# Hybrid decoder trunk: constant matmuls ahead of the first data, two weight groups in one walk, and upper weights against both parts of the activations in one matmul

## The chip, the core and the metric

The kernel runs on one core of a Trainium2 chip. The metric is device time in microseconds of that core; the median of three runs is given. TensorE (PE) multiplies, VectorE (DVE) and ScalarE (ACT) do the elementwise work, GpSimd (POOL) a little of it, and SyncE (SP) issues nearly all transfers. A profile is one execution, recorded by the hardware.

## What is computed

One layer over 256 tokens of width 2048, in float32, with three branches that are gated and merged:

```python
h = rmsnorm(x, ln_in_g)
proj = h @ w_in                                   # 2048 x 19472
conv_a, conv_b, conv_z, q, k, v, gla_z, alpha_lr, mq, mz, gate_pre = split(proj)
u = causal_depthwise_conv(conv_a * sigmoid(conv_b), dw_w, dw_b)        # 31 taps
u = silu(layernorm(u)) * silu(conv_z);  y_conv = u @ w_conv_out + b_conv_out
log_a = log_sigmoid(alpha_lr @ w_alpha2 + b_alpha) / 16
o = rmsnorm(gla_chunked(q * 256**-0.5, k, v, log_a))                   # 4 heads
y_gla = (o * silu(gla_z)) @ w_gla_out
om = softmax(mq @ mk.T * 128**-0.5) @ mv          # 4 heads, 256 memory tokens
y_mem = (om * silu(mz)) @ w_mem_out
g = sigmoid(gate_pre + b_gate)
out = rmsnorm(x + (g0 * y_conv + g1 * y_gla + g2 * y_mem) @ w_out)
```

## The kernel before, in words

**Products.** Weights and activations are each split into an upper part of 12 significant bits (`hi`, `xh`) and the rest (`lo`, `xl`), both as fp32r; a product is three matmuls, upper by upper, upper by lower and lower by upper (`mm3`, L157 to L160). Weights come in groups of 512 columns, 53 groups in all, in the order in which they are used. A group is walked in chunks of two k (tiles of 128 features), 512 KB each (`chunks`, `chunk`): one transfer on SP's queue into one of four `raw` tiles, a cast on ACT to `hi` (L140), a subtraction on DVE to `lo` (L141), five tiles of each. These three are put ahead of other work in the order (`high_priority`).

**Two kinds of group.** `group_n` (tokens on partitions) has activations as the stationary operand and 512 columns of weights moving: 96 matmuls of 512 columns. `group_t` (features on partitions, tiles named pt_...) has 128 columns of weights stationary and the 256 tokens moving: for each k and each of four feature tiles a triple of 256 columns, 192 matmuls, summed in two PSUM tiles [128, 2, 256]. PSUM has five such tiles for the groups (`mm_tile`) and three for the rest (`aux_tile`). The 19 transposed groups are conv a and b (four times, `conv_group`), q and k (twice, `qk_group`), the memory's keys mk, and mq and mz (`memory_groups`), and the four of conv z (`gated_conv`). What uses a finished group reads the PSUM tile directly, 512 columns at a time.

**Activations.** `raw_operand` loads xt (features on partitions, 2 MB) four tiles at a time as the first group asks for them, on SP's queue between the weights, and splits each with the gain of the norm (L187, L188). The first four groups, conv a 0, conv b 0 and q and k of the first half, use these not yet normalized activations (XR), and their results are multiplied by `xrb`, the tokens' 1/rms, which a side task (`x_norm`) makes from squares meanwhile. From v on, the normalized X is used (`xh`, `xl`). The first group starts with two chunks of one k (256 KB). The constants `idents` and `tap` are loaded on SP after conv a 0 (L457 to L459).

**Order.** Everything between the groups (the 480 tap steps of the convolution, L359, the four heads, the memory attention, the norms) is a generator that is advanced at each chunk (`tick`), with a credit of 1.2 a tick; the order on TensorE is written at the end of the kernel. From this program order and the priorities a planner fixes each engine's order before the run. It may bring later work of an engine forward when what stands ahead isn't ready by its own clock.

## Time and profile before

| | us |
|---|---|
| median of three runs | 1248.16 |
| lowest and highest run | 1247.41, 1248.22 |
| span of the profiled execution | 1246.8 |
| PE busy in it | 1231.0 |
| DVE busy in it | 964.0 |
| ACT busy in it | 591.8 |

The span runs from the first to the last instruction; a run's time has about 1.4 us more around it. Each matmul has a record; the time from one start to the next is what it costs in a row of matmuls, and its recorded duration is longer, since matmuls overlap. A matmul on plain float32 has two records.

### The profile page before, as it was taken

Reading aid. Unit: us, or ns where it says so; the run is one execution under the profiler, and the core shown is the slowest. Engines: PE = TensorE matmul, PEld = TensorE weight load, DVE = VectorE, ACT = ScalarE, POOL = GpSimd, SP = SyncE. Lnnn points to the kernel's source line nnn. Section 1 sums busy time; section 2 is a strip of 40 time slices with the busy share of each in tenths; the row PEclk is TensorE's granted clock in tenths of the full one; section 3 lists DMA queues with packets and bytes.
Section 4 is the critical chain, followed back from the end, with each engine's and each line's share of the span. In section 5 each row is a group of like instructions: output and inputs, shape, how many; then the busy total and the mean of one; then the engine's idle time right before and its main releaser. Section 6 shows DMA issues by size and latency. Waiting matters only on the chain.

```text
span 1246.8 us, 18825 instructions
## 1 busy us (share of the span) xinstructions
PE 1231.0 (99%) x7338; PEld 1093.9 (88%) x7338; DVE 964.0 (77%) x1502; ACT 591.8 (47%) x711; POOL 18.6 (1%) x29
## 2 busy tenths in 40 slices
PE   7999999999999999999999999999999999999997
PEld 7999899988998998889988888888999888888885
DVE  7999999699999667999699979964565554655553
ACT  7534676446553454444445445544354444444442
POOL 0000000000020000000000000000000000000000
PEclk9999999999999999999999999999999999999999
DMA  7565745446545445665465555565555655567562
GB/s 272 186 191 170 236 153 195 155 161 221 188 165 193 159 152 183 205 204 193 161 218 171 200 201 171 179 228 194 195 183 190 202 202 195 205 227 268 187 215 71
DMA packets 71672, 238.37 MB, mean 191 GB/s; under 512 B 7792, under 2 KB 12144, under 8 KB 71584
## 3 DMA queue, kind: packets, MB, share of 16 engines
q1 hardware_dynamic: 71440, 237.13, 56.6%
q8 instruction: 57, 0.93, 0.3%
q14 instruction: 31, 0.25, 0.1%
q10 hardware_dynamic: 144, 0.05, 0.0%
HBM read 235.06 MB, written 2.10 MB: 190 GB/s over the span
## 4 chain that ended last, share of the span: by engine, by line
PE 97%; DMA 1%; DVE 1%; issue 0%; SPq 0%; ACT 0%; POOLq 0%; DVEq 0%; POOL 0%
PE pt_cb L158 2%; PE pt_cz L158 2%; PE pt_cb L159 2%; PE pt_cb L160 2%; PE pt_cz L159 2%; PE pt_cz L160 2%; PE pn_gc L159 2%; PE pn_gm L159 2%; PE pn_gz L158 2%; PE pn_go L159 2%; PE pn_go L158 2%; PE pn_gm L158 2%; PE pn_gz L159 2%; PE pn_yo L158 2%; PE pn_go L160 2%; PE pn_gc L160 2%
## 5 line engine op out<-in xcount | busy, mean ns | idle before, releaser
L359 DVE SCALAR_TENSOR_TENSOR conv<-u,tap,conv 128x256 f32<-128x256 f32 x480 | 207.3, 474 | 0.0
L158 PE MATMUL pt_ca<-xh,hi_ca 128*128 128x256 f32 x256 | 72.7, 289 | 6.1 <-ACT xh L187 5.1
L159 PE MATMUL pt_ca<-xl,hi_ca 128*128 128x256 f32 x256 | 73.5, 288 | 0.2
L160 PE MATMUL pt_ca<-xh,lo_ca 128*128 128x256 f32 x256 | 72.7, 287 | 0.9 <-DVE lo_ca L141 0.9
L158 PE MATMUL pt_cb<-xh,hi_cb 128*128 128x256 f32 x256 | 72.4, 283 | 0.0
L141 DVE TENSOR_TENSOR lo_yc<-raw_yc,hi_yc 128x1024 fp32r<-128x1024 f32 x32 | 39.2, 1225 | 42.9 <-ACT hi_yc L140 42.9
L160 PE MATMUL pt_cz<-xh,lo_cz 128*128 128x256 f32 x256 | 71.9, 281 | 0.0
L158 PE MATMUL pt_cz<-xh,hi_cz 128*128 128x256 f32 x256 | 71.9, 281 | 0.0
L159 PE MATMUL pt_cz<-xl,hi_cz 128*128 128x256 f32 x256 | 71.9, 281 | 0.0
L160 PE MATMUL pt_cb<-xh,lo_cb 128*128 128x256 f32 x256 | 71.8, 282 | 0.0
L159 PE MATMUL pt_cb<-xl,hi_cb 128*128 128x256 f32 x256 | 71.8, 281 | 0.0
L141 DVE TENSOR_TENSOR lo_cz<-raw_cz,hi_cz 128x1024 fp32r<-128x1024 f32 x32 | 39.2, 1224 | 35.7 <-ACT hi_cz L140 35.7
L141 DVE TENSOR_TENSOR lo_gc<-raw_gc,hi_gc 128x1024 fp32r<-128x1024 f32 x32 | 39.1, 1223 | 34.2 <-ACT hi_gc L140 34.2
L141 DVE TENSOR_TENSOR lo_out<-raw_out,hi_out 128x1024 fp32r<-128x1024 f32 x32 | 39.0, 1224 | 31.5 <-ACT hi_out L140 31.2
L140 ACT CAST hi_gc<-raw_gc 128x1024 fp32r<-128x1024 f32 x32 | 33.6, 1052 | 50.3 <-PE pn_yc L160 24.9
L140 ACT CAST hi_yc<-raw_yc 128x1024 fp32r<-128x1024 f32 x32 | 33.7, 1053 | 49.5 <-PE pn_gc L160 33.4
L140 ACT CAST hi_yo<-raw_yo 128x1024 fp32r<-128x1024 f32 x32 | 33.6, 1051 | 46.7 <-PE pn_go L160 23.4
L141 DVE TENSOR_TENSOR lo_yo<-raw_yo,hi_yo 128x1024 fp32r<-128x1024 f32 x32 | 38.8, 1221 | 21.6 <-ACT hi_yo L140 21.6
L158 PEld LDWEIGHTS pt_ca<-xh,hi_ca 128*128 128x128 f32 x256 | 49.5, 196 | 6.4 <-ACT xh L187 5.1
L140 ACT CAST hi_gm<-raw_gm 128x1024 fp32r<-128x1024 f32 x32 | 33.6, 1050 | 45.2 <-PE pn_gm L160 24.6
L140 ACT CAST hi_go<-raw_go 128x1024 fp32r<-128x1024 f32 x32 | 33.7, 1052 | 44.6 <-PE pn_yo L160 24.6
L140 ACT CAST hi_cz<-raw_cz 128x1024 fp32r<-128x1024 f32 x32 | 33.6, 1050 | 44.3 <-PE pt_cz L159 36.0
(352 smaller groups left out, 4108.9 us busy)
## 6 DMA issues: line engine op xcount, KB each, us to landing
raw_cb<-in_weights SPq DMA_DIRECT2D x32, 512.0 KB, 3.5
raw_gm<-in_weights SPq DMA_DIRECT2D x32, 512.0 KB, 3.2
raw_gz<-in_weights SPq DMA_DIRECT2D x32, 512.0 KB, 3.3
raw_go<-in_weights SPq DMA_DIRECT2D x32, 512.0 KB, 3.6
raw_yo<-in_weights SPq DMA_DIRECT2D x32, 512.0 KB, 3.2
raw_cz<-in_weights SPq DMA_DIRECT2D x32, 512.0 KB, 3.2
raw_gc<-in_weights SPq DMA_DIRECT2D x32, 512.0 KB, 3.2
raw_yc<-in_weights SPq DMA_DIRECT2D x32, 512.0 KB, 3.2
```

Source lines behind the costliest of these rows:

```text
L140: nc.scalar.copy(hi, raw)
L141: nc.vector.tensor_sub(lo, raw, hi.bitcast(F32))
L158: nc.tensor.matmul(o, lhsT=ah, rhs=bh, start=first, stop=False, skip_group_check=True)
L159: nc.tensor.matmul(o, lhsT=ah, rhs=bl, start=False, stop=False, skip_group_check=True)
L160: nc.tensor.matmul(o, lhsT=al, rhs=bh, start=False, stop=last, skip_group_check=True)
L359: nc.vector.scalar_tensor_tensor(acc, u[:, i, j:j + T], tap[:, c, j:j + 1], acc, op0=ALU.mult, op1=ALU.add)
```

## The change

Four things are done.

1. Nine matmuls of a constant tile with itself are put first on TensorE; nothing reads their result. The load of the per-feature vectors gets the same priority.
2. x is loaded at once at the start, in five transfers on ACT's queue; `idents` and `tap` go to POOL's queue.
3. The first two groups, conv a 0 and conv b 0, are walked together (`group_pair`): a chunk is one k of both, 512 KB, for 24 matmuls of 256 columns, into four PSUM tiles.
4. The other 17 transposed groups are walked in two halves of 256 columns, each in four chunks of four k (512 KB again). The two parts of an activation tile lie side by side (`xs`), and the upper weights meet both in one matmul of 512 columns; the lower weights meet the upper part in one of 256. A PSUM tile then holds for one feature tile two sums, which `total` adds: a copy on ACT and an addition on DVE, at the end of each half, before the former use. In conv groups b now comes before a, so that the gate is ready when a is. The scale of q is put into the copies of v.

```diff
-NU, LAG, HELD, XWAIT = 2, 2, 12, 4
+NU, LAG, HELD, XWAIT = 2, 2, 12, 5
+WARM = 9
...
-    def chunks(w, cols, nk, acts, name, first=CK, spare=False):
+    def chunks(w, cols, nk, acts, name, first=CK, spare=False, size=CK):
         if not isinstance(cols, list):
             cols = [(cols, GC)]
         k = 0
         while k < nk:
-            ck = min(CK, first) if k < 2 * first else CK
+            ck = min(size, first) if k < 2 * first else size
...
-    def group_t(w, c0, acts, nk, name, first=CK):
-        pss = [mm_tile(f"pt_{name}_{j}") for j in range(2)]
-        for k, hi, lo, ah, al in chunks(w, c0, nk, acts, name, first):
-            for n in range(4):
-                cols = slice(n * P, (n + 1) * P)
-                mm3(pss[n // 2][:, (n % 2) * T:(n % 2 + 1) * T], hi[:, cols], lo[:, cols], ah, al,
+    def group_t(w, c0, acts, nk, name, use):
+        for h in range(2):
+            pss = [mm_tile(f"pt_{name}_{2 * h + j}") for j in range(2)]
+            cols = [(c0 + h * GC // 2, GC // 2)]
+            for k, hi, lo, ah, al, both in chunks(w, cols, nk, acts, f"{name}_{h}", 2 * CK, size=2 * CK):
+                for n in range(2):
+                    c = slice(n * P, (n + 1) * P)
+                    nc.tensor.matmul(pss[n], lhsT=hi[:, c], rhs=both, start=k == 0, stop=False,
+                                     skip_group_check=True)
+                    nc.tensor.matmul(pss[n][:, 0:T], lhsT=lo[:, c], rhs=ah, start=False, stop=k == nk - 1,
+                                     skip_group_check=True)
+            for n in range(2):
+                use(2 * h + n, pss[n][:, 0:T], pss[n][:, T:2 * T])
+    def group_pair(w, c0, c1, acts, nk, name):
+        pss = [mm_tile(f"pt_{name}_{j}") for j in range(4)]
+        cols = [(c0, GC), (c1, GC)]
+        for k in range(nk):
+            hi, lo = chunk(w, k, 1, cols, f"{name}_{k}")
+            ah, al, _ = acts(k)
+            for n in range(8):
+                c = slice(n * P, (n + 1) * P)
+                mm3(pss[n // 2][:, (n % 2) * T:(n % 2 + 1) * T], hi[:, 0, c], lo[:, 0, c], ah, al,
                     k == 0 and n % 2 == 0, k == nk - 1)
-        return [p.rearrange("p (a b) -> p a b", a=2) for p in pss]
+            tick()
+        pss = [p.rearrange("p (a b) -> p a b", a=2) for p in pss]
+        return pss[:2], pss[2:]
...
     ones = const.tile([P, P], F32, name="ones")
-    nc.gpsimd.memset(ones, 1.0)
+    vec = const.tile([P, NVEC], F32, name="vec")
+    with tc.high_priority(offset=2 * AHEAD):
+        nc.gpsimd.memset(ones, 1.0)
+        nc.scalar.dma_start(vec, vecs)
+        pw = aux_tile("warm_pe")
+        for _ in range(WARM):
+            nc.tensor.matmul(pw[:, 0:P], lhsT=ones, rhs=ones, start=True, stop=True, skip_group_check=True)
     warm = tp.tile([P, 1], F32, name="warm", tag="st")
     nc.scalar.activation(warm, ones[:, 0:1], AF.Sigmoid)
-    vec = const.tile([P, NVEC], F32, name="vec")
-    nc.scalar.dma_start(vec, vecs)
...
-        hi, lo, raw, rest = [], [], [], []
+        both, raw, rest = [], [], []
+        def load(i, a, b, queue):
+            f = 4 * i * P
+            queue.dma_start(raw[i][:, a:b, :], src[f + a * P:f + b * P, :].rearrange("(k p) c -> p k c", p=P))
         def part(i, a, b):
-            f = 4 * i * P
-            nc.sync.dma_start(raw[i][:, a:b, :], src[f + a * P:f + b * P, :].rearrange("(k p) c -> p k c", p=P))
+            if not keep:
+                load(i, a, b, nc.sync)
             for j in range(a, b):
                 kk = 4 * i + j
-                split_scaled(raw[i][:, j, :], vec[:, v0 + kk:v0 + kk + 1], hi[i][:, j, :], lo[i][:, j, :])
+                split_scaled(raw[i][:, j, :], vec[:, v0 + kk:v0 + kk + 1], both[i][j][:, 0, :], both[i][j][:, 1, :])
+        def ahead():
+            with tc.high_priority(offset=AHEAD):
+                for i in range(4):
+                    raw.append(b4([P, 4, T], f"{name}r{i}"))
+                    for a, b in ((0, 1), (1, 4)) if i == 0 else ((0, 4),):
+                        load(i, a, b, nc.scalar)
         def acts(k):
             i, j = k // 4, k % 4
-            if i == len(raw):
-                raw.append(b4([P, 4, T], f"{name}r{i}"))
-                hi.append(b4([P, 4, T], f"{name}h{i}", F32R))
-                lo.append(b4([P, 4, T], f"{name}l{i}", F32R))
+            if i == len(both):
+                if not keep:
+                    raw.append(b4([P, 4, T], f"{name}r{i}"))
+                pairs = [b4([P, 2, 2, T], f"{name}s{i}_{n}", F32R) for n in range(2)]
+                both.append([pairs[n // 2][:, n % 2] for n in range(4)])
...
-            return hi[i][:, j, :], lo[i][:, j, :]
-
-        return acts, raw
-
-    xh = const.tile([P, KT, T], F32R, name="xh")
-    xl = const.tile([P, KT, T], F32R, name="xl")
+            return parts(both[i][j])
+        return acts, raw, ahead
+    xs = const.tile([P, KT, 2, T], F32R, name="xs")
+    def parts(both):
+        return both[:, 0, :], both[:, 1, :], both.rearrange("p a b -> p (a b)")
     def X(k):
-        return xh[:, k, :], xl[:, k, :]
-
-    XR, xraw = raw_operand(xt, V_LN, "x", True)
-    MR, mraw = raw_operand(memt, V_MLN, "m", False)
+        return parts(xs[:, k])
+    XR, xraw, load_x = raw_operand(xt, V_LN, "x", True)
+    MR, mraw, _ = raw_operand(memt, V_MLN, "m", False)
...
     def conv_group(g, acts, rb=None):
-        pa = group_t("w_in", C_A + g * GC, acts, KT, f"ca{g}", CK if rb is None else 1)
-        if g == 0:
-            load_constants()
-        pb = group_t("w_in", C_B + g * GC, acts, KT, f"cb{g}")
         u = tp.tile([P, 4, TAPS - 1 + T], F32, name=f"u{g}", tag="u", bufs=NU)
         nc.gpsimd.memset(u[:, :, 0:TAPS - 1], 0.0)
-        for j in range(2):
-            sg = t2([P, 2, T], f"sg_{g}_{j}")
-            ua = u[:, 2 * j:2 * j + 2, TAPS - 1:]
-            if rb is None:
-                nc.scalar.activation(sg, pb[j], AF.Sigmoid)
-                nc.vector.tensor_mul(ua, pa[j], sg)
-            else:
-                rbb = rb.unsqueeze(1).to_broadcast([P, 2, T])
+        if rb is None:
+            sg = [t2([P, 2, T], f"sg_{g}_{j}") for j in range(2)]
+            def gate(f, a, b):
+                s = sg[f // 2][:, f % 2, :]
+                total(s, a, b)
+                nc.scalar.activation(s, s, AF.Sigmoid)
+            def gated(f, a, b):
+                uf = u[:, f, TAPS - 1:]
+                total(uf, a, b)
+                nc.vector.tensor_mul(uf, uf, sg[f // 2][:, f % 2, :])
+            group_t("w_in", C_B + g * GC, acts, KT, f"cb{g}", gate)
+            group_t("w_in", C_A + g * GC, acts, KT, f"ca{g}", gated)
+        else:
+            pa, pb = group_pair("w_in", C_A + g * GC, C_B + g * GC, acts, KT, f"cab{g}")
+            rbb = rb.unsqueeze(1).to_broadcast([P, 2, T])
+            for j in range(2):
+                sg = t2([P, 2, T], f"sg_{g}_{j}")
+                ua = u[:, 2 * j:2 * j + 2, TAPS - 1:]
...
+    def total(out, a, b):
+        nc.scalar.copy(out, a)
+        nc.vector.tensor_add(out, b, out)
...
-        nc.sync.dma_start(idents, ident_in)
-        nc.sync.dma_start(tap, taps)
+        nc.gpsimd.dma_start(idents, ident_in)
+        nc.gpsimd.dma_start(tap, taps)
...
-        rbb = None if rb is None else rb.unsqueeze(1).to_broadcast([P, 2, T])
-        pq = group_t("w_in", C_Q + g * GC, acts, KT, f"q{g}")
-        q = b4([P, 4, T], f"q{g}")
-        for j in range(2):
-            qj = q[:, 2 * j:2 * j + 2, :]
-            if rb is None:
-                nc.scalar.activation(qj, pq[j], AF.Copy, scale=DKH ** -0.5)
-            else:
-                nc.vector.scalar_tensor_tensor(qj, pq[j], DKH ** -0.5, rbb, op0=ALU.mult, op1=ALU.mult)
-        pk = group_t("w_in", C_K + g * GC, acts, KT, f"k{g}")
-        k = b4([P, 4, T], f"k{g}")
-        for j in range(2):
-            kj = k[:, 2 * j:2 * j + 2, :]
-            if rb is None:
-                nc.scalar.copy(kj, pk[j])
-            else:
-                nc.vector.tensor_mul(kj, pk[j], rbb)
-        return q, k
+        made = []
+        for c0, n in ((C_Q, "q"), (C_K, "k")):
+            t = b4([P, 4, T], f"{n}{g}")
+            def use(f, a, b):
+                total(t[:, f, :], a, b)
+                if rb is not None:
+                    nc.vector.tensor_mul(t[:, f, :], t[:, f, :], rb)
+            group_t("w_in", c0 + g * GC, acts, KT, f"{n}{g}", use)
+            made.append(t)
+        return made
...
-                nc.scalar.copy(v[:, t, :], pv[t])
+                nc.scalar.activation(v[:, t, :], pv[t], AF.Copy, scale=DKH ** -0.5)
...
-            pz = group_t("w_in", C_Z + g * GC, X, KT, f"cz{g}")
-            hi.append(b4([P, 4, T], f"uh{g}", F32R))
-            lo.append(b4([P, 4, T], f"ul{g}", F32R))
-            for j in range(2):
-                s = silu_psum(pz[j], f"cz{g}_{j}")
-                f = slice(2 * j, 2 * j + 2)
-                nc.vector.tensor_mul(s, s, conv[g][:, f, :])
-                split(s, hi[g][:, f, :], lo[g][:, f, :])
+            uh, ul = b4([P, 4, T], f"uh{g}", F32R), b4([P, 4, T], f"ul{g}", F32R)
+            hi.append(uh)
+            lo.append(ul)
+            z = [t2([P, 2, T], f"cz{g}_{j}") for j in range(2)]
+            def use(f, a, b):
+                total(z[f // 2][:, f % 2, :], a, b)
+                if f % 2:
+                    zj, fs = z[f // 2], slice(f - 1, f + 1)
+                    silu(zj, f"cz{g}_{f}")
+                    nc.vector.tensor_mul(zj, zj, conv[g][:, fs, :])
+                    split(zj, uh[:, fs, :], ul[:, fs, :])
+            group_t("w_in", C_Z + g * GC, X, KT, f"cz{g}", use)
...
+    load_x()
+    load_constants()
     norm = start(x_norm())
     tapsk = [conv_group(0, XR, xrb)]
     q, k = qk_group(0, XR, xrb)
```

## Rows read from the trace of the kernel before

**Rows 1.** The page's head and part 1: busy us, share, instructions of TensorE.

```profile
span 1246.8 us, 18825 instructions
...
PE 1231.0 (99%) x7338; PEld 1093.9 (88%) x7338; DVE 964.0 (77%) x1502; ACT 591.8 (47%) x711; POOL 18.6 (1%) x29
```

**Rows 2.** All waits of PE: who waited for whom, total us, times, longest.

```profile
PE pt_ca L158 <- ACT xh L187: 5.1, 1, 5.1
...
PE pt_ca L160 <- DVE lo_ca L141: 0.9, 1, 0.9
```

**Rows 3.** Windows: us, busy of PE, PEld, DVE, ACT, POOL, clock, DMA, GB/s.

```profile
59.20:376.50 317.30, 317.30 (x2365) 300.94 (x2364) 298.36 (x578) 171.83 (x219) 12.01 (x8) 1.00 0.56 184
376.50:480.50 104.00, 104.00 (x666) 93.67 (x665) 75.20 (x131) 46.39 (x64) 1.38 (x3) 1.00 0.50 170
```

**Rows 4.** Windows over whole groups: pt_q, pt_cz (four), pn_go, pn_yo.

```profile
59.20:82.20 23.00, 23.00 (x194) 23.00 (x193) 21.56 (x35) 9.64 (x10) 0.00 (x0) 1.00 0.68 220
882.00:972.40 90.40, 90.40 (x769) 90.40 (x768) 52.12 (x54) 40.86 (x45) 0.00 (x0) 1.00 0.55 187
838.20:860.20 22.00, 22.00 (x97) 18.05 (x97) 12.17 (x13) 8.38 (x8) 0.00 (x0) 1.00 0.56 194
860.20:881.90 21.70, 21.70 (x97) 17.97 (x96) 10.90 (x11) 9.48 (x10) 0.00 (x0) 1.00 0.57 194
```

**Rows 5.** Timeline of PE (start, duration, what): first and last of nine.

```profile
249.78 0.28 PE L158 MATMUL pt_k<-xh,hi_k 128*128 128x256 f32 x1
...
250.68 0.28 PE L160 MATMUL pt_k<-xh,lo_k 128*128 128x256 f32 x1
```

**Rows 6.** The critical chain: start, us, what; the norm's broadcast, two float32 matmuls.

```profile
43.44 0.44 PE bc_x L208 x4
```

**Rows 7.** Timeline of the first 15 us: an x issue, and single matmul starts.

```profile
3.60 0.43 SPq L256 DMA_DIRECT2D xr<-in_xt  x1
...
5.07 0.79 PE L158 MATMUL pt_ca<-xh,hi_ca 128*128 128x256 f32 x2 [5.07 <-ACT xh L187]
...
13.94 0.41 PE L158 MATMUL pt_ca<-xh,hi_ca 128*128 128x256 f32 x1
...
14.15 0.41 PE L159 MATMUL pt_ca<-xl,hi_ca 128*128 128x256 f32 x1
...
14.88 0.28 PE L160 MATMUL pt_ca<-xh,lo_ca 128*128 128x256 f32 x1
...
14.99 0.28 PE L158 MATMUL pt_ca<-xh,hi_ca 128*128 128x256 f32 x1
```

**Rows 8.** Windows of the start: matmuls up to 14.6, and transfers.

```profile
5.00:14.60 9.60, 8.52 (x37) 8.02 (x38) 6.24 (x11) 6.03 (x12) 0.00 (x0) 1.00 1.00 362
...
2.00:4.00 2.00, 0.00 (x0) 0.00 (x0) 0.00 (x0) 0.67 (x3) 0.00 (x0) 1.00 0.87 280
4.00:6.00 2.00, 0.93 (x3) 0.72 (x4) 1.09 (x2) 1.01 (x2) 0.00 (x0) 1.00 0.91 322
```

**Rows 9.** Groups by line: out<-in, shape, count, busy us, mean ns, idle before.

```profile
L140 ACT CAST hi_cz<-raw_cz 128x1024 fp32r<-128x1024 f32 x32 | 33.6, 1050 | 44.3 <-PE pt_cz L159 36.0 <-PE pn_yo L160 8.3
...
L629 ACT COPY v<-pn_va 128x264 f32<-128x264 f32 x2 | 0.7, 379 | 0.4 <-PE pn_va L160 0.4
...
L710 DVE COPY om<-om 128x256 f32<-128x256 f32 x4 | 1.7, 416 | 0.0
...
L341 DVE TENSOR_TENSOR u<-pt_ca,sg 128x512 f32<-128x512 f32 x6 | 4.1, 683 | 0.6 <-ACT sg L340 0.6
```

**Rows 10.** Timelines of DVE, ACT and PE: casts and emptying around q and k.

```profile
63.28 1.28 DVE L346 TENSOR_TENSOR u<-pt_ca,sg 128x512 f32<-128x512 f32 x2
...
214.30 1.05 ACT L140 CAST hi_k<-raw_k 128x1024 fp32r<-128x1024 f32 x1 [1.66 <-PE pt_q L159]
...
223.42 0.28 PE L158 MATMUL pt_k<-xh,hi_k 128*128 128x256 f32 x1
...
232.41 1.08 ACT L605 ACTIVATE q<-pt_q 128x512 f32<-128x512 f32 x2
```

## What the change should do to the time

> **What bounds the kernel now.** I read the page's first lines, then the waits of PE, then windows by stage, then single starts. TensorE is busy 1231.0 of 1246.8 us [rows 1]. Its only waits are three, from 5.1 down to 0.9 us, all for the first group, pt_ca [rows 2]; after that it issues one matmul behind the other, and the run is the sum of the intervals between matmul starts. VectorE is the next engine: 298.4 us of work in the 317.3 us from 59.2 to 376.5, then 75.2 in 104.0 [rows 3]. So a gain has two sources: the start, and the interval of a matmul.
>
> The intervals: where features lie on partitions, 768 matmuls of 256 columns (pt_cz) take 90.4 us, 117.7 ns each; in pt_q, on the not yet normalized activations, 192 take 23.0 us, 120 ns each. Where tokens lie on partitions, 96 matmuls of 512 columns take 22.0 us (pn_go) and 21.7 us (pn_yo), 229 and 226 ns [rows 4]. Two matmuls of 256 cost 235 ns, one of 512 costs 226 to 229, so some 8 ns seem to go with each instruction. Not everywhere: in part of pt_k eight intervals take 0.90 us, 113 ns each [rows 5], just half of pn_yo's 226.
>
> **Part 1, fewer and wider matmuls.** Each of the 17 transposed groups that stay (19 less the two that now walk together) has 64 triples of (feature tile, k). A triple was three matmuls of 256; it becomes one of 512 (upper weights by both parts side by side) and one of 256. The columns stay 768, one instruction and one weight load go. The trace has no 512 beside a 256 with weights as the stationary operand, so bounds: the high end is 226 + 113 = 339 ns against 353 now, 14 ns less; the low end is a 512 that costs two of 256, 0 less. Below zero is excluded by the rows: no 512 row is slower than 2 x 117.7. I take 345 (227.5 + 117.7), 8 ns less, the sum of the two plain rows. Eleven groups at 353: 11 x 64 x 8 = 5.6 us. Two groups at 360 (q and k of the first half), 11 ns less, as half of the excess may belong to their operand: 1.4. Four groups where part of the intervals may be 113 already, as in pt_k (q, k and the two of conv 2), 4 ns less: 1.0. Sum 8.0 us, ends 0 and 16 (14 ns on 15 groups, 21 on two).
>
> The Trainium skill (TensorE: Matmul & The Clock Gate, section "Wait — 56ns, not 53.3ns?") gives each matmul a fixed cost of about 2.5 ns at 2.4 GHz; by that part 1 would bring 17 x 64 x 2.5 = 2.7 us, an estimate from that page. By it, 113 and 226 agree better than 117.7 and 229.
>
> **Part 2, the start.** Up to 59.2 us two groups are done: 384 matmuls at 0.12 = 46.1 us, and about 1.0 for the norm's small matmuls (0.44 for four records of bc_x [rows 6], as much again for fs_x and the restarts). So 59.2 - 47.1 = 12.1 us are lost: 5.1 before the first matmul, then half clock. The granted-clock column reads 1.00 throughout here, but the starts are 0.21 us apart at 14 us and 0.11 at 14.9 [rows 7, 8]: the 1.2 GHz level, then 2.4. From 5.0 to 14.6 lie 37 matmuls [rows 8], 37 x 0.093 = 3.5 us lost, and 3.5 remain for gaps in which weights or activations were late.
>
> After: the first chunk is 512 KB instead of 256 KB, beside x, which is now issued at once from ACT's queue, and the constants from POOL's. The stretch from 2 to 4 us moved 0.56 MB, the one to 6 us 0.64 MB [rows 8]. If the chunk gets half of that, it is whole when 1.05 MB are, at 5.5 us; with a cast of 1.05 us [rows 9] the first real matmul is at 6.7 (bounds 5.5, the chunk first in line, and 9, all in equal parts). The nine constant matmuls are of bc_x's form: 0.22 us each at full clock, 0.44 at half, so 4 us from about 1.0 to 5.0. They stand in front of data that isn't there; if it came sooner they would cost the difference. Whether the clock is up by the first real matmul no row shows: between 0 lost and the 3.5 of now I take 1.0, since the engine works from 1.0 instead of 5.1. Gaps: a chunk now feeds 24 matmuls, 2.9 us of PE, instead of half of that, and x is wanted half as fast, so I take 0.8. Loss 6.7 + 1.0 + 0.8 = 8.5, gain 3.6 us, ends 0 (first matmul at 8.5, 2.6 of half clock, 1 of gaps) and 6.4.
>
> The five x issues on ACT's queue take 0.43 us each [rows 7], 2.2 in all, ahead of the table load and the first cast; they are through before 5.5, when the data lands. SP loses the x and constant issues between its weight issues; POOL has little to do there, and idents is first read for bc_x at 43. The Trainium skill (DMA: Bandwidth & Descriptors, section "Issuing engines are not separate DMA queues") says that another issuing engine saves issue time only. That speaks against a gain from the second queue; my sum counts none, only the denser use of each byte.
>
> **Part 3, what is added.** Each feature tile now needs a copy out of PSUM on ACT (0.38 us, by the 264-column copy) and an add on DVE (0.42, by the 256-column copy out of PSUM) [rows 9]. On DVE: 3.7 us more for each of three conv groups (8 adds, 4 multiplications of 0.42 instead of 2 of 0.68), 2.0 for each of q and k of the first half, 1.7 for a plain group: some 30 us over the run, 16 of them between 59 and 376, where 298.4 + 16.2 = 314.6 us meet 317.3 - 9 x 0.5 = 312.8 of PE time. That is more than all of it; the 2 us in excess, and 4 that the shorter start pushes in, run on into the 29 us that DVE has idle until 480 [rows 3]. It costs nothing as long as what slips is the taps and the heads' side work, not the low parts of the weights. The side work's ticks stay eight to a group (16 instead of 17 in the first two), and the scale of q only moves into v's copies: nothing.
>
> The added waits: the copy waits for the last matmul of its half group; behind it in ACT's queue stands the next cast, for which DVE and then PE wait. The casts run far ahead: one for pt_k begins at 214.3, pt_k's matmuls at 223.4 [rows 10]. The other wait is for PSUM: four of five tiles are held by two half groups, so the third half needs the first emptied, 11 us later, or 16.5 if its first feature tile (16 x 345 ns) goes ahead alone. Emptying was late by up to 9 us: pt_k took over from pt_q at 223.4, and pt_q's tiles were read at 232.4 [rows 10]. So it is covered. The joint pair holds four tiles as well; the first comes free by the multiplication that begins at 63.3 [rows 10], 4.7 us after 59.2 at its end, and q's first feature tile covers 5.5. For these edges I take 1.0 us, ends 0 and 6.
>
> **Sum.** 1246.8 - 3.6 - 8.0 + 1.0 = 1236.2 us of span. The median of the runs lies 1.4 above the span of the profiled execution, so 1237.6 us.
>
> **The rivals.**
> A, the interval goes with the columns, as 113 and 226 say: part 1 brings 1.4 at most by the two groups at 120, the start stays: 1248.2 - 3.6 - 1.4 + 1.0 = 1244.2 us. For it: [rows 5] and pn_yo. Against: 117.7 for all four groups of pt_cz. (The 2.5 ns of the Trainium skill's TensorE: Matmul & The Clock Gate, same section, would make it 1242.9.)
> B, the weight load is what makes a 256 slower than 113, and the 512 hides it: 339 ns a triple, part 1 brings 15, and the time is 1230 us. For it: pn_yo shows no excess over twice 113. Against: pn_go has 229.
> C, the start brings nothing (a first chunk twice as large, the clock up no earlier): 1241.2 us.
> D, slower: late emptying of PSUM. The place is the stretch from 59 to 376, where DVE has little idle time left; emptying needs an ACT and a DVE step for each feature tile, in orders that are fixed in advance. From a lateness of 11 us on (16.5 if the first tile goes ahead alone) PE pays each us at each of the 18 halves there; at 13 us late that is 2 x 18 = 36 us, less the gain of 10.6: 1274 us; at 12 us late 1256. For it: the 9 us seen, and DVE at 94% there. Against: seen once, and PE never waits there today.
>
> **Chances.** Forecast 0.48 (its own range 1233 to 1241), A 0.18, B 0.13, C 0.11, D 0.10. Faster by over 0.2%, which is under 1245.7 and about what a measurement of this kernel can tell: the forecast, B, C and most of A, 0.83. The rest of A and its mixtures with C: same, 0.08. D, less its mildest forms: slower, 0.09. The range leaves out D and the far ends of A and B: 1229 to 1246.
>
> **What would show it.** In the changed profile: 128 matmuls in a transposed group instead of 192, in 22.1 us (pt_cz's four: 88.3; 90 would be A, 86.8 B). Starts 0.12 apart from the first real matmul on, and that at 6 to 7 us; the joint pair done by 55.6 us (59 is C). No wait of PE after it; a wait of a matmul for an ACT copy or a DVE add out of PSUM, in any half from 59 to 376, is D. I would be wrong, too, if DVE's added work held up the low parts of the weights.

## The result, and the profile of the changed kernel

The changed kernel takes 1258.92 us (1258.24 to 1259.17), the kernel before 1247.79 us beside it: ratio 1.0091, 95% interval 1.0078 to 1.0104. It is 11.1 us slower; the forecast was 10.6 us faster.

The first lines of the page answer to [rows 1]: the span is 1257.3 us, and PE has fewer instructions and is busy longer.

```profile
span 1257.3 us, 16832 instructions
...
PE 1235.9 (98%) x6268; PEld 1048.0 (83%) x6268; DVE 989.2 (79%) x1578; ACT 610.0 (49%) x781; POOL 17.9 (1%) x31
```

The waits of PE (line waited for, total, times, longest) answer to [rows 2]: the first is 6.0 us instead of 5.1, but now comes *after* the constant matmuls, and there are new ones for the norm of x, for a copy of pn_mv, for the heads (pl and po are tiles of theirs) and for an addition that empties pt_q (pt_k <- DVE q).

```profile
PE pt_cab L159 <- ACT xs L211: 6.0, 1, 6.0
PE fs_x L240 <- DVE pq_x L253: 2.9, 1, 2.9
PE pt_mq L173 <- ACT mv L709: 1.4, 1, 1.4
...
PE pt_cab L161 <- DVE lo_cab L142: 0.5, 1, 0.5
PE pl L580 <- DVE on L657: 0.4, 1, 0.4
PE pt_k L173 <- DVE q L455: 0.3, 1, 0.3
PE po L649 <- DVE sX L638: 0.2, 1, 0.2
```

The start by windows answers to [rows 8]. The columns are PE, PEld, DVE, ACT and POOL busy (with instructions), granted clock, DMA share and GB/s.

```profile
6.00:10.00 4.00, 0.00 (x0) 0.00 (x0) 1.93 (x2) 3.35 (x4) 0.00 (x0) 1.00 1.01 382
20.00:26.00 6.00, 6.00 (x53) 6.00 (x52) 6.00 (x6) 6.00 (x12) 0.00 (x0) 1.00 0.03 8
26.00:30.00 4.00, 0.99 (x8) 0.70 (x6) 4.00 (x10) 1.86 (x2) 0.00 (x0) 1.00 0.00 0
32.00:34.00 2.00, 2.00 (x12) 2.00 (x12) 1.87 (x3) 0.00 (x0) 1.18 (x1) 0.54 0.91 311
```

PE has nothing from 5.2 to 11.2 us although the DMA engines are full. At 12 us the matmuls start 0.21 us apart, at 18 us 0.12:

```profile
12.25 0.41 PE L160 MATMUL pt_cab<-xs,hi_cab 128*128 128x256 f32 x1
12.46 0.41 PE L161 MATMUL pt_cab<-xs,lo_cab 128*128 128x256 f32 x1
...
17.95 0.28 PE L159 MATMUL pt_cab<-xs,hi_cab 128*128 128x256 f32 x1
18.07 0.28 PE L160 MATMUL pt_cab<-xs,hi_cab 128*128 128x256 f32 x1
```

The clock column reads 1.00 at both, so here too it is the spacing that tells the level. From 20 to 30 us DMA is all but idle, PE idles for 3 us of the last four, and then the clock is at its lower level again. The pair is done and pt_q begins at 66.1 us, in the kernel before at 59.2. What ACT did meanwhile (start, time in all, operation, tiles, count; ACTq is its DMA issuing):

```profile
2.15 0.86 ACTq L284 DMA_DIRECT2D xr<-in_xt  x1
4.86 0.37 ACTq L284 DMA_DIRECT2D xr<-in_xt  x1
5.26 1.28 ACT L141 ACT_TABLE_LOAD   x1 [5.26 <-DMA vec<-in_vecs]
5.32 2.85 ACTq L284 DMA_DIRECT2D xr<-in_xt  x1
6.55 1.04 ACT L141 CAST hi_cab<-raw_cab 128x1024 fp32r<-128x1024 f32 x1
8.22 1.04 ACT L141 CAST hi_cab<-raw_cab 128x1024 fp32r<-128x1024 f32 x1 [0.62 <-issue]
9.28 1.28 ACT L266 ACT_TABLE_LOAD   x1
...
10.68 0.49 ACT L211 ACTIVATE xs<-xr,vec 128x256 fp32r<-128x256 f32 x1
...
15.77 2.94 ACT L249 ACTIVATE sq_x<-xr 128x1024 f32<-128x1024 f32 x3
...
20.80 3.29 ACT L211 ACTIVATE xs<-xr,vec 128x256 fp32r<-128x256 f32 x8
23.99 1.98 ACT L141 CAST hi_cab<-raw_cab 128x1024 fp32r<-128x1024 f32 x2
```

All five issues together (count, then min/median/max in ns and the first and last start):

```profile
L284 ACTq DMA_DIRECT2D xr<-in_xt x5: 374/457/2852, 1.2 to 5.3; - x5
```

The first three are through at 3.0; the fourth begins at 4.86, just after the load of the vectors (vec) has landed at 4.8, for which the table load behind it waits as well; the fifth takes 2.85 and ends at 8.17. So issues and wait hold ACT's queue from 1.2 to 8.2 us, 5.0 of them issuing; the 6.9 us of the expectations below have the wait counted in. The table of functions is loaded twice, and the first split of x is over at 11.2. Then the squares and splits of *all* of x go ahead of the casts of chunks 4 and 5, which begin at 24.0. VectorE does the same: its reductions of the squares run from 17.2 to 25.4, the low part of chunk 4 follows at 29.14.

The four groups of pt_cz, where nothing is late, answer to [rows 4] (90.40 us for 768 matmuls); the window is of pt_cz's instructions alone:

```profile
892.20:982.70 90.50, 90.41 (x512) 78.49 (x512) 5.90 (x14) 5.25 (x15) 1.00 0.62 187
```

A third fewer instructions, the same time. Single starts in that stretch show how it comes:

```profile
900.06 0.40 PE L173 MATMUL pt_cz<-xs,hi_cz 128*128 128x512 f32 x1
900.29 0.28 PE L175 MATMUL pt_cz<-xs,lo_cz 128*128 128x256 f32 x1
900.41 0.40 PE L173 MATMUL pt_cz<-xs,hi_cz 128*128 128x512 f32 x1
```

The 512 takes 0.23 to the next start, the 256 0.12, the pair of them 0.35: three times 117.7 ns. A table of where the profiled executions stand to that of before (start of the group, less its start before, in us; negative is earlier) shows where the time went. Here pt_q and pn_va are those of the first half of the heads, pn_v (v2) is the second half's; conv 1 and conv 2 are the second and third of the four conv groups; last is the last matmul. Rows below the changed kernel are experiments, told further down. Each row is one execution. That of the kernel before is a long one, with a span of 1246.8 us where the median of the later runs is 1245.8, so the rows look up to 1.0 us better than the medians do; that of x_on_sp is the lowest of its four (1251.21 to 1254.12), that of start_only the highest (1252.76 to 1255.43).

| kernel | pt_q | pn_va | pn_v (v2) | conv 2 | pn_mv | pt_mz | pt_cz | last |
|---|---|---|---|---|---|---|---|---|
| changed | 6.9 | 6.0 | 7.6 | 8.4 | 8.7 | 10.3 | 10.3 | 10.3 |
| start_only | 6.4 | 6.4 | 6.4 | 6.4 | 6.5 | 6.3 | 6.3 | 6.3 |
| groups_only | -0.5 | -1.3 | 0.0 | 0.9 | 1.1 | 2.7 | 2.8 | 2.8 |
| groups_split | -0.5 | -0.5 | -0.1 | 0.5 | 0.4 | 0.4 | 0.6 | 0.6 |
| groups_split_no_add | -0.6 | -0.6 | -1.9 | -1.4 | -1.4 | -1.5 | -1.4 | -1.4 |
| x_on_sp | -3.6 | -3.9 | 1.1 | 1.2 | 1.1 | 2.7 | 2.5 | 2.5 |
| x_on_sp_no_add | -2.5 | -2.8 | -1.2 | -0.3 | -0.1 | -0.1 | -0.4 | -0.4 |
| pair_sp | -2.9 | -2.8 | -2.9 | -2.9 | -2.8 | -2.8 | -2.9 | -2.9 |

In the changed kernel 6.9 us are lost by 66 us, 0.9 won back in pt_q and pt_k of the first half, 4.3 lost again up to pt_mz, and nothing after it.

### The profile page after: what moved, and what is told of

It is laid out like the page before. It is cut to its first block, busy times and chain, and to the rows that moved or that the text cites. A ratio compares the mean times of both kernels' runs of the same rounds, so it can differ in the third digit from the quotient of the medians.

```text
span 1257.3 us, 16832 instructions
## 1 busy us (share of the span) xinstructions
PE 1235.9 (98%) x6268; PEld 1048.0 (83%) x6268; DVE 989.2 (79%) x1578; ACT 610.0 (49%) x781; POOL 17.9 (1%) x31
## 4 chain that ended last, share of the span: by engine, by line
PE 96%; DVE 1%; ACT 1%; issue 1%; DMA 0%; ACTq 0%; POOLq 0%; DVEq 0%; POOL 0%
PE pt_cz L173 5%; PE pt_ca L173 4%; PE pt_cb L173 4%; PE pt_cz L175 2%; PE pt_k L173 2%; PE pt_q L173 2%; PE pn_go L159 2%; PE pn_gm L160 2%; PE pn_gc L160 2%; PE pn_gz L160 2%; PE pn_go L160 2%; PE pn_gz L161 2%; PE pn_gc L161 2%; PE pn_gm L159 2%; PE pn_yo L159 2%; PE pn_go L161 2%
## 5 line engine op out<-in xcount | busy, mean ns | idle before, releaser
L173 PE MATMUL pt_cz<-xs,hi_cz 128*128 128x512 f32 x256 | 90.5, 397 | 0.0
L175 PE MATMUL pt_cz<-xs,lo_cz 128*128 128x256 f32 x256 | 71.9, 281 | 0.0
L173 PE MATMUL pt_cb<-xs,hi_cb 128*128 128x512 f32 x192 | 68.0, 398 | 0.0
L173 PE MATMUL pt_ca<-xs,hi_ca 128*128 128x512 f32 x192 | 67.5, 399 | 0.0
L173 PEld LDWEIGHTS pt_cz<-xs,hi_cz 128*128 128x128 f32 x256 | 48.1, 188 | 11.9
L141 ACT CAST hi_yc<-raw_yc 128x1024 fp32r<-128x1024 f32 x32 | 33.7, 1053 | 49.5 <-PE pn_gc L161 33.4
L142 DVE TENSOR_TENSOR lo_go<-raw_go,hi_go 128x1024 fp32r<-128x1024 f32 x32 | 39.2, 1224 | 22.2 <-ACT hi_go L141 22.1
L141 ACT CAST hi_out<-raw_out 128x1024 fp32r<-128x1024 f32 x32 | 33.5, 1054 | 44.2 <-PE pn_out L161 29.7
L141 ACT CAST hi_gz<-raw_gz 128x1024 fp32r<-128x1024 f32 x32 | 33.7, 1052 | 41.9 <-PE pn_gz L161 31.4
L175 PE MATMUL pt_cb<-xs,lo_cb 128*128 128x256 f32 x192 | 53.7, 281 | 0.0
L175 PE MATMUL pt_ca<-xs,lo_ca 128*128 128x256 f32 x192 | 52.1, 282 | 0.0
```

Source lines behind the costliest of these rows:

```text
L141: nc.scalar.copy(hi, raw)
L142: nc.vector.tensor_sub(lo, raw, hi.bitcast(F32))
L173: nc.tensor.matmul(pss[n], lhsT=hi[:, c], rhs=both, start=k == 0, stop=False, skip_group_check=True)
L175: nc.tensor.matmul(pss[n][:, 0:T], lhsT=lo[:, c], rhs=ah, start=False, stop=k == nk - 1, skip_group_check=True)
```

## The experiments

Each ratio is to the kernel before on the same chip, with its 95% interval.

**Does the merged matmul bring anything?** split512, from the changed kernel:

```
-  nc.tensor.matmul(pss[n], lhsT=hi[:, c], rhs=both, start=k == 0, ...)
+  nc.tensor.matmul(pss[n][:, 0:T], lhsT=hi[:, c], rhs=both[:, 0:T], start=k == 0, ...)
+  nc.tensor.matmul(pss[n][:, T:2 * T], lhsT=hi[:, c], rhs=both[:, T:2 * T], start=False, ...)
```

> The changed kernel with each 512-column matmul of the transposed groups written as two of 256 columns again, on the same operands and the same halves of PSUM (192 matmuls a group instead of 128); all else as changed. Theory 'columns' (the interval of a matmul goes with its columns, the merged instruction saves nothing): pt_cz's four groups stay at 90.3 us and the time stays within 1.5 us of the changed kernel's 1258.9. Theory 'instruction' (8 ns go with each matmul, as forecast): 17 x 64 x 8 = 8.7 us more, 1267.6, and pt_cz at 92.3. A gain would mean that the merged form itself costs something.

1256.85 us, ratio 1.0074 (1.0059 to 1.0089): 2 us *less* than the changed kernel. pt_cz in split512:

```profile
889.70:980.20 90.50, 90.44 (x768) 90.43 (x768) 5.88 (x14) 5.33 (x15) 1.00 0.56 187
```

90.44 against 90.41 us: the interval goes with the columns, theory 'columns'. That it got faster by more than 1.5 us, neither theory expected. Part of it is seen in pt_cb of conv 1, first the changed kernel, then split512, each a window over the group's own instructions:

```profile
158.00:180.60 22.60, 22.60 (x128) 19.53 (x128) 0.83 (x2) 0.73 (x2) 1.00 0.45 140
```

```profile
159.10:180.90 21.80, 21.74 (x192) 21.80 (x192) 0.84 (x2) 0.74 (x2) 1.00 0.43 142
```

Here the 192 matmuls of 256 go at 113 ns, and the merged ones at the equal of 117.7.

**Which half of the change loses?** Two runs share the change out. groups_only has the start of before and the changed groups behind it; start_only has the new start and the old groups. Their cores:

```
groups_only, from the changed kernel (cut)
-            pa, pb = group_pair("w_in", C_A + g * GC, C_B + g * GC, acts, KT, f"cab{g}")
+            pa = group_one("w_in", C_A + g * GC, acts, KT, f"ca{g}", 1)
+            load_constants()
+            pb = group_one("w_in", C_B + g * GC, acts, KT, f"cb{g}")
...
-    load_x()
-    load_constants()
start_only, from the kernel before (cut)
-        pa = group_t("w_in", C_A + g * GC, acts, KT, f"ca{g}", CK if rb is None else 1)
+            pa, pb = group_pair("w_in", C_A + g * GC, C_B + g * GC, acts, KT, f"cab{g}")
...
+    load_x()
+    load_constants()
```

> The half groups of 512 + 256 columns and the totals out of PSUM as changed, for every group but the first two, but the start as before: the first two groups one after the other, the first chunks of one feature tile by 512 columns, x issued from SP when it is asked for, constants from SP, no constant matmuls. Theory 'two separate losses' (6.9 us lie in the start, 3.5 to 4.5 in the stretch from 223 to 437 us, where emptying and restarts cost): 1251 to 1253, 59.2 us at the end of the first two groups. Theory 'one loss' (the later start pushes side work into the middle, and that is what costs there): 1246 to 1248. The forecast's own terms would have given 1248.2 - 8 + 1 = 1241.

> The kernel before with the new start alone: constant matmuls, x issued at once from ACT's queue, constants from POOL's, the first two groups walking together with one chunk for both; all the other groups as before (three matmuls of 256 columns, read out of PSUM in pairs). Theory 'two separate losses': 1247.8 + 6.9 = 1254.7 (1253.5 to 1256), the pair done at 66 us, first real matmul at 11. Theory 'one loss': the middle is lost as well, 1258 to 1259. The forecast had 1244.

groups_only 1251.30 us, ratio 1.0031 (1.0020 to 1.0041), so +3.9; start_only 1254.75 us, ratio 1.0055 (1.0040 to 1.0070), so +7.3. Together 11.2 against 11.1: two separate losses. The waits of groups_only after its start are those of the changed kernel: pl, pt_k and po with the same 0.4, 0.3 and 0.2, and this one:

```profile
PE pt_mq L172 <- ACT mv L697: 1.4, 1, 1.4
```

**What in the half groups costs 3.9?** no_add leaves out VectorE's addition in the totals:

```
         nc.scalar.copy(out, a)
-        nc.vector.tensor_add(out, b, out)
```

> The run with the half groups and the start of before (1251.3 us), whose totals out of PSUM leave out VectorE's addition: ACT copies the first half alone, so the sums lack the product of upper weights and lower activations, and VectorE has some 27 us less to do. Theory 'VectorE' (the heads' small matmuls, in PE's order, wait for a VectorE that is full from 190 to 260 us): the stretch from the start of pt_k of conv 2 to the start of pn_v goes from 34.7 back to 32.7 and the time to 1248 to 1249.5; the wait of pt_mq for the copies of pn_mv on ACT (1.4) stays. Theory 'restarts' (more and shorter groups, and the intervals of 113 ns that are lost): nothing changes, 1250.5 to 1251.5.

1249.23 us, ratio 1.0013 (1.0004 to 1.0023), 2.1 less. Most of pt_k (from 222.9, after one early matmul) and the side work in it now take 33.3 us up to pn_v instead of 34.7, and the waits for VectorE in it are gone. Yet from pn_va to pn_v the run takes 0.7 us more than groups_only: a wait of 1.1 for a cast came in pt_ca. The wait of 1.4 of pt_mq, which was to stay, went. So the size fits 'VectorE', and the place does not: every edit makes the planner write new orders, and only the total is to be trusted. Two more runs ask whether the prices add up: the split of split512 on groups_only, with and without that addition.

> The half groups and totals with the start of before (1251.3 us), but with the 512-column matmul written as two of 256 on the same operands. Theory 'two prices' (the merged form costs 2.1, VectorE's additions 2.1): 1249.2 (1248.7 to 1249.8). Theory 'one price' (the gain of the split in the other start was a shift of the side work that happened there alone): 1251, and more than 2 us of waits between 190 and 260 us.

> As before it, and without VectorE's addition in the totals (ACT copies the first half alone, so the sums lack the product of upper weights and lower activations). Theory 'two prices': 1251.3 - 2.1 - 2.1 = 1247.1, the kernel before within 0.6 us. Theory 'one price': 1249.2, as without the addition alone.

1249.08 us, ratio 1.0012 (1.0003 to 1.0021), and 1247.32 us, ratio 0.9997 (0.9988 to 1.0006). By the totals, two prices: 2.2 for the merged form, 1.8 for the additions; without both, the half groups, ACT's copies and the order of the gates cost nothing in sum. In this pair the place fits too: from the start of pt_k to pn_v 34.9 us with the additions, 33.2 without.

The 2.2 are not all intervals. Taken from the single starts in the 17 groups, 256 columns take 117.64 ns on average before, 117.66 in groups_only and 117.22 in groups_split: merged, nearly every group stands at 117.4 to 117.8, where q and k of the first half and pt_mk were at 120 and parts of conv 1, conv 2 and the second q and k at 113. Over 17 x 192 intervals the 0.44 ns are 1.4 us, an estimate; against the kernel before they are nothing. What is left goes with the wait of pt_mq, and that is a matter of the order, since no_add loses it with the merged form kept. The table shows that groups_split no longer loses between pn_mv and pt_mz, where groups_only waits for the copies of pn_mv out of PSUM; PE in groups_only, with the start, the time and the wait in front:

```profile
421.88 1.02 PE L640 MATMUL po<-v,s 128*128 128x512 f32 x2
424.25 0.50 PE L172 MATMUL pt_mq<-xs,hi_mq 128*128 128x512 f32 x1 [1.36 <-ACT mv L697]
```

and what ACT did before it:

```profile
421.22 0.60 ACT L643 ACTIVATE osq<-po 128x512 f32<-128x512 f32 x1 [6.25 <-PE po L637]
...
422.93 0.60 ACT L643 ACTIVATE osq<-po 128x512 f32<-128x512 f32 x1 [1.03 <-PE po L640]
...
423.52 1.26 ACT L697 ACTIVATE mv<-pn_mv,rs_m 128x512 f32<-128x512 f32 x2
```

pn_mv ended at 400.9; ACT reads it 23 us later, because in its order the copies stand behind the squares of a head's output, for which it idles 6.25 and 1.03 us until PE has made them. In the kernel before the two copies ran at 416.1 and nobody waited for them. It is a late emptying of PSUM, the mechanism of rival D, at one place.

**What in the start costs 7.3?** Four runs from the changed kernel. x_on_sp issues x from SP, when it is asked for:

```
-            if not keep:
-                load(i, a, b, nc.sync)
+            load(i, a, b, nc.sync)
...
-    load_x()
```

> The changed kernel with x issued from SP when it is asked for, as in the kernel before (the planner then also puts the one load of the function table first on ACT, and three chunks' casts ahead of the squares of x); the pair, its 512 KB chunks, constant matmuls and half groups stay. Theory 'ACT's queue' (five issues of x, 6.9 us of ACT's time, and a second table load stand ahead of the first split): first real matmul at 6.5 to 7.5, the pair done at 57 to 61 us, 1251 to 1254. Theory 'data' (the first chunk of twice the size beside x is what comes late): first real matmul after 8.5, the pair done at 63 or later, 1256 or more.

1252.56 us, ratio 1.0041 (1.0026 to 1.0056). The first real matmul goes at 5.92 us, and the pair is done (pt_q begins) at 55.6. ACT in that run:

```profile
1.19 1.28 ACT L266 ACT_TABLE_LOAD   x1 [1.19 <-PEq L1006]
...
4.42 1.04 ACT L141 CAST hi_cab<-raw_cab 128x1024 fp32r<-128x1024 f32 x1 [1.73 <-DMA raw_cab<-in_weights]
5.37 0.50 ACT L211 ACTIVATE xs<-xr,vec 128x256 fp32r<-128x256 f32 x1
```

x_lazy_act has x asked for in the same way, but on ACT's queue; x_early_sp has all of x at once, as in the change, but on SP's; early_table keeps the change and only puts the first sigmoid, with its table load, ahead of the issues.

```
x_lazy_act, from x_on_sp
-            load(i, a, b, nc.sync)
+            load(i, a, b, nc.scalar if keep else nc.sync)
x_early_sp, from the changed kernel
-                        load(i, a, b, nc.scalar)
+                        load(i, a, b, nc.sync)
```

> The changed kernel with x still issued from ACT's queue, but four feature tiles at a time, when they are asked for, instead of all at the beginning. Theory 'ACT's queue' (an x issue holds ACT up by 0.4 to 2.9 us wherever it stands, and the second table load comes back with it): first real matmul at 8.5 to 10, but no long gap at 26 to 30 us, the pair done at 57 to 60, 1253.5 to 1256. Theory 'all at once' (what costs is only that x and with it the squares of the norm come ahead of the chunks' casts): as from SP, first real matmul at 6 to 6.5, pair done at 55.5 to 57, 1252 to 1253.

> The changed kernel with all of x issued at the beginning as in the change, but from SP's queue (the planner then puts the first three x issues ahead of the first chunk, and the splits and squares of x ahead of nearly all casts). Theory 'all at once': the casts of the chunks wait behind the squares on ACT and their low parts behind the reductions on VectorE; first real matmul after 8, PE starved again between 10 and 30 us, the pair done at 62 or later, 1256 to 1262. Theory 'ACT's queue' (only the issuing engine matters): the pair done by 58, 1252 to 1254.

> The changed kernel with the first sigmoid, which brings the load of ACT's function table, put ahead of the issues on ACT: one table load instead of two, x still issued from ACT. If the five issues on ACT's queue are what holds up the first split, the first real matmul stays late, at 9.5 to 10.5 us (the second table load and the sigmoid, 1.3 us, are saved once), and the time is 1256.5 to 1258.5. If the second table load is the main cause: first real matmul at 7 or before and 1254 or less.

x_lazy_act 1253.95 us, ratio 1.0052 (1.0038 to 1.0066), first real matmul at 8.5, pair done at 57.7. x_early_sp 1261.68 us, ratio 1.0112 (1.0098 to 1.0125), first at 12.1, pair done at 68.9. early_table 1258.74 us, ratio 1.0090 (1.0076 to 1.0104), first at 9.5, pair done at 65.5. So the queue is the smaller part: with x asked for in time, it costs 2.1 us by the end of the pair (57.7 against 55.6). At the end the medians differ by 1.4 (1253.95 less 1252.56), but the four runs of x_on_sp lie between 1251.21 and 1254.12, and the profiled x_lazy_act lost 1.5 more in pt_k under a lower clock (last section), so its price there is not resolved. Asking for all of x at once costs 5.0 on ACT's queue (1258.92 less 1253.95) and 9.1 on SP's (1261.68 less 1252.56), since it brings the squares and reductions in front of the weights, and on SP three issues of x in front of the first chunk as well. That also explains early_table: PE starts 1.7 us sooner and then waits for casts (1.6) and the norm (1.6); 0.2 us arrive at the end. That another issuing engine saves issue time only, the forecast had taken from the Trainium skill (DMA: Bandwidth & Descriptors, section "Issuing engines are not separate DMA queues"). The traces agree as far as the bytes go: 382 GB/s from 6 to 10 us with ACT issuing x, 409 in x_on_sp.

**Do the constant matmuls help?** x_on_sp_nowarm takes them out of x_on_sp; before_warm puts nine into the kernel before and changes nothing else.

> The run with x issued from SP (1252.6 us), without its constant matmuls. Theory 'spared half clock': the first 9 to 10 us of the pair's matmuls go 0.21 apart again, the pair ends 2 to 3.6 us later than 55.5, and 1254.5 to 1256. Theory 'the constant matmuls do nothing' (the pair's gain comes from one chunk feeding 24 matmuls): 55.5 us and 1252.6.

> The kernel before with the nine constant matmuls alone. Theory 'spared half clock' (the clock counts PE's work from 1.0 us on, so that the first group's matmuls start 0.12 apart at once): up to 3.5 us less, of which late data gives some back: 1244 to 1246, starts 0.12 apart at 8 us. Theory 'data' (in the first group PE waits for chunks and x anyway, a faster PE only waits longer): 1247 to 1248.

x_on_sp_nowarm 1252.96 us, ratio 1.0049 (1.0035 to 1.0062). At its start it does what 'spared half clock' says: 0.21 apart until 10.9 us (with them 0.12 from 6.2 on), the pair done at 57.5. At the end it can't be told from x_on_sp: its four runs lie between 1252.43 and 1255.72. before_warm 1247.67 us, ratio 1.0000 (0.9991 to 1.0009): 0.12 apart from 7.0 us instead of 14.8, but then PE waits 2.8 us in two places for low parts of chunks from VectorE, and the first two groups end 0.9 sooner in the profile, no more than the profiled kernel before is long: theory 'data'.

**Where does the early pair's gain go?** x_on_sp is 3.6 us ahead at pt_q and behind from pn_v on. PE in x_on_sp at the start of pt_k's side work:

```profile
233.23 0.71 PE L578 MATMUL pl<-d 128*128 128x128 f32 x4 [1.56 <-DVE on L655]
235.24 0.50 PE L173 MATMUL pt_k<-xs,hi_k 128*128 128x512 f32 x1 [1.29 <-DVE q L453]
```

The first wait is a head's. The second is for the addition that reads pt_q out of PSUM: emptying is late here too.

> The run with x issued from SP (1252.6 us), whose totals leave out VectorE's addition: ACT copies the first half alone, so the sums lack the product of upper weights and lower activations. Theory 'VectorE is full': the stretch from the start of pt_k of conv 2 to the start of pn_v goes from 38.5 to 34 us or less, the early pair's gain arrives at the end, 1246 to 1248.5. Theory 'order': that stretch stays above 36.5 and the time above 1250.

1248.47 us, ratio 1.0007 (0.9997 to 1.0016), 4.1 us less than x_on_sp by the medians, 2.9 between the two profiled executions; from pt_k, one early matmul left out, to pn_v 33.4 us instead of 38.5. The same 11 us, first x_on_sp, then without the addition (columns as above):

```profile
225.00:236.00 11.00, 7.51 (x36) 5.11 (x35) 10.56 (x38) 4.91 (x14) 1.87 (x2) 1.00 0.24 86
```

```profile
225.00:236.00 11.00, 10.62 (x58) 8.36 (x57) 9.96 (x32) 4.49 (x13) 0.74 (x2) 1.00 0.34 110
```

In x_on_sp VectorE has no gap from 190 to 225 us (in the kernel before it has 3.0 us of them from 216 to 225), and then PE stands still for 3.5 us, because the next instruction in PE's order is a head's and then one that needs pt_q emptied; with the additions out, PE stands for 0.4. So the additions are the cause. But VectorE has no gap from 190 to 225 us without them either: that it is full is not enough, and whether what helps is the work that is gone or the other order that the planner writes without it was not separated.

**A version that beats both.** pair_sp is start_only with x on SP, asked for in time: constant matmuls, the pair, old groups. pair_sp_w11 has eleven constant matmuls.

> The kernel before with three parts of the change alone: the constant matmuls, the first two groups walking together with one chunk for both, and constants on POOL's queue; x stays on SP, issued when it is asked for, and all other groups stay as before (three matmuls of 256 columns, no totals out of PSUM). Theory 'additive' (the start gains its 3.6 us once ACT issues no x, the half groups and totals are the other loss and are absent): the pair done at 55.5 us and 1247.5 - 3.6 = 1243.9 (1243 to 1245), faster than both kernels. Theory 'side work moves the gain away' (what the start gains is lost between 190 and 260 us, where the heads' small matmuls wait for VectorE, with or without totals): 1246 to 1248.

> The fastest so far (1246.1 us: the pair, constant matmuls, x from SP, other groups as before) with eleven constant matmuls instead of nine, so that they end at 6.1 us, where the first real one can go. Its matmuls stood 0.21 apart until 10.2 us; in the run with constant matmuls and no break after them that ended at 7.0. Theory 'unbroken work': 0.12 apart from about 7 us, 1.0 to 1.6 us less, 1244.5 to 1245.1. Theory 'the clock rises when it rises' or 'data': the same 1246.1, or 0.2 more.

pair_sp 1246.06 us, ratio 0.9988 (0.9979 to 0.9997); pair_sp_w11 1245.73 us, ratio 0.9987 (0.9978 to 0.9996). Both are faster than the kernel before, by 1.5 to 1.7 us, and than the changed one by 13. The table speaks for 'additive' (2.9 us ahead at pt_q and at the end), the median for less (1.5). Of the difference, 1.0 is the long profiled execution of the kernel before: against the median span of 1245.8, pair_sp's 1244.1 is 1.7 less. With eleven, the matmuls go 0.12 apart from 6.8 us instead of 10.2, but PE waits 0.5 to 0.7 for a cast, a split of x and low parts, four times: theory 'data'.

## Why the prediction was wrong

**What bounds the kernel** was read rightly: without waits, the time is the sum of PE's intervals. What was missing is that PE's order holds the heads' matmuls too, so whoever feeds them is on the path as soon as it is full.

**Part 1** failed in the term of 8 ns for an instruction: -8.0 forecast, while the intervals of the 17 groups came out as before (117.66 against 117.64 ns), and the merged form cost 2.2 against the same half groups unmerged (groups_only less groups_split). The step was to compare a 256 with features on partitions (117.7 ns) with a 512 that has another stationary operand (227.5) and to give the difference to the instruction. In one stream a 512 takes 235 ns and a 256 takes 118. Rival A was right for the interval; [rows 5] were its evidence, and I gave it 0.18. By the rule of the Trainium skill (TensorE: Matmul & The Clock Gate, section "Wait — 56ns, not 53.3ns?") 256 matmuls fewer in pt_cz would be 0.6 us less, an estimate; the rows show 0.03. The bound "below zero is excluded" failed as well: no row of 512 was slower than 2 x 117.7, but the stream it replaces can run at 113, as pt_cb of split512 does. The two groups at 120 gained, 0.85 us in all against 1.4 forecast, and pt_mk too; what stood at 113 lost as much.

**Part 2**, 3.6 us of gain, measured 7.3 of loss. It failed at the step that the five x issues "take 0.43 us each" and "are through before 5.5". SP's price nearly held for four of them on ACT (0.37 to 0.86), but the fourth began only at 4.86, and the fifth took 2.85 and ended at 8.17. So ACT's first cast began at 6.55 instead of 4.42 in x_on_sp, a second cast, ahead of the split, waited for the last issue, and the second table load, 1.28 us, I did not see coming: the first split began at 10.68 instead of 5.37. The larger omission is in the gaps: x wanted "half as fast" was counted as 0.8 us of gaps; x *loaded* all at once moved squares and reductions ahead of the casts, and cost more than the queue. With x on SP the pair is done at 55.6, as forecast, but that is partly luck: the first matmul came at 5.9 (forecast 6.7), hardly anything went at half clock (forecast 1.0), and the gaps took some 2.5 us (forecast 0.8; 55.6 less 47.1 and 5.9). The clock term was half right: where the first real matmul came 0.7 us after the last constant one (x_on_sp), the 0.12 began at 6.2; where it came 1.0 us after (pair_sp), at 10.2; after the 6.0 us wait of the changed kernel the matmuls stood 0.21 apart until 16.7 us.

**Part 3** was +1.0; the additions alone cost 1.8 with the start of before and 4.1 with an early pair (by medians; 2.9 between the profiled executions). I had computed that VectorE's work exceeds the stretch's time (314.6 against 312.8 us) and then let the excess slip at no cost "as long as what slips is the taps and the heads' side work". Heads' side work is just what PE waits for. Rival D's mechanism shows twice in the changed kernel, pt_mq's wait of 1.4 us and pt_k's of 0.3 for pt_q's addition (1.3 in x_on_sp), instead of 36 us; before pt_mq's wait PE went on for 22 us after pn_mv's end, more than the 16.5 named.

**The sum** of the measured parts is 7.3 + 2.2 + 1.8 = 11.3 against 11.1. The slower side had 0.09, for D without its mildest forms; no rival said that the start itself could lose.

## What to carry to other kernels

When a transfer is moved to an engine that also computes, price its issues from that engine's own rows, one by one and with the waits between them, and look at what the earlier data lets the planner put ahead of the weights. Before fewer, wider matmuls are counted as a gain, find one stretch in which two widths run with the same operands. An engine whose added work fills a stretch isn't free because its work is "side work": ask whose in-order queue that side work stands in.

## What the runs showed of the hardware

The interval of a matmul of 256 columns has levels rather than a spread: 113, 117.7 and 120 ns, each kept over long stretches, whole groups among them. split512 ran pt_cb of conv 1 at 113 and pt_cz at 117.7, the same operation on the same kind of operands. Within pt_k of the kernel before the level changes between 117.7 and 113 where matmuls of the heads come in between. In the changed kernel's transposed groups nearly every 512 took 235, two of the middle level. What chooses the level is open, and it was not tried.

An x issue took 0.43 us on SP [rows 7]; on ACT four took 0.37 to 0.86, and the fifth, with the others under way, 2.85, and ACT's next cast began 0.05 after its end.

PE's granted clock fell in mid-run. In the profiled x_on_sp_nowarm (1255.72 us, the slowest of its four) PE worked 2.26 and 2.90 of 4 us from 232 to 240, and the clock column went to its 1.2 GHz level (0.53):

```profile
232.00:236.00 4.00, 2.26 (x11) 1.32 (x9) 3.56 (x12) 3.02 (x12) 1.86 (x2) 1.00 0.00 0
236.00:240.00 4.00, 2.90 (x9) 2.52 (x10) 4.00 (x15) 1.73 (x4) 0.54 (x1) 0.53 0.00 0
```

In x_on_sp PE worked 4.76 of the 8 us from 228 to 236, and the clock column stayed at 1.00. The profiled x_lazy_act fell too (0.76 from 236 to 240, 0.82 to 244). So a wait of PE can cost more than its own length: pt_k up to pn_v took 41.1 us in x_on_sp_nowarm and 40.0 in x_lazy_act against 38.5. The four runs of x_on_sp stand in two pairs 2.5 us apart (1251.21 and 1251.37, 1253.76 and 1254.12); whether the clock fell in the slower pair no trace shows.
